# PLE gate and FFN gate/up products as seven half-size block products, with weight sums made by accumulating transfers, and the residual formed during the merge

## The chip, the core and the metric

The kernel runs on one core of a Trainium2 chip. The metric is the device time of one launch in microseconds, as a median of timed runs. The engines that matter are TensorE (PE, matrix products; its weight loads are shown as PEld), VectorE (DVE), ScalarE (ACT), GpSimd (POOL), and SyncE (SP), which here only issues transfers.

## The reference, cut to what matters

One transformer block on 512 tokens of width 1024, in fp32. After a layer norm, a gated MLP and a gated linear recurrence (HGRN2) run side by side and are merged; what the change touches is the tail:

```python
h1  = layer_norm(ALPHA * h + mix, ln1_g, ln1_b)                  # h = layer_norm(x, ln0), 512 x 1024
hid = silu(h1 @ w_ffn_gate) * (h1 @ w_ffn_up)                    # two 1024 x 2816 weights
ffn = hid @ w_ffn_down                                           # 2816 x 1024
ple = sigmoid(h1 @ w_ple_gate + b_ple_gate) * (p @ w_ple)        # 1024 x 1024 gate
out = layer_norm(ALPHA * h1 + ffn + ple, ln2_g, ln2_b)
```

## The kernel before

Each operand of a product is an exact sum of two fp32r parts, a high part h and a low part l, and each product is three matmuls (h·h, h·l, l·h). A weight arrives as a "raw" tile of 128 x 1024 values (512 KB, one SP transfer); ACT casts it to the high part (`wh`), and DVE subtracts to get the low part (`wl`). `split` does these two steps and `load_unit` the load and the split. Raw tiles have three buffers, so a load waits until an earlier tile's split is done.

The stages follow each other: the start, HGRN2, the gated MLP, the merge (`mwa`, `mwb`, `mga`, `mgb`), the output projection with layer norm 1 (`wo`, `ps_wo`), the PLE gate (`pg`, `ps_pg`), the FFN gate/up products (`fg` and `fu`, `ps_fg` and `ps_fu`) and the down product (`ps_d`) with layer norm 2. Around the change:

- LN1: the residual `r1 = ALPHA * LN0(x)` is formed on DVE at the head of the output projection, from a fresh load of x (`xr`, L676 to L680). When a token tile is normed, `turn` transposes it on PE (`ps_h`, L700) and splits it into `h1h`, `h1l`.
- PLE gate: for two column halves and four token tiles, eight k-steps of three matmuls, with 512 columns moving; 192 matmuls in all.
- FFN gate/up: the loop over m covers 256 columns of each of the two weights. `gemm_a` keeps a 128 x 128 block of weight stationary and moves 512 tokens: 48 matmuls for gate and 48 for up per m, 11 m's, 1056 matmuls. ACT makes the silu (`fsg`), DVE the product (`fhf`), and the split into `hidh`, `hidl` follows at once.
- Down: eleven k-pairs, whose operands `hidh`, `hidl` are there already.

Each engine runs its instructions in one fixed order, which a scheduler sets at build time; no engine overtakes its own queue, and that holds for the transfers that SP and POOL issue.

Of the kernel before, what the change touches and what calls it, by code (L numbers as in the profile page):

```python
# [8 lines left out]
F32 = mybir.dt.float32  # L9
F32R = mybir.dt.float32r  # L10
# [16 lines left out]
# columns of the input projection  # L27
# [4 lines left out]
def block_kernel(  # L32
# [50 lines left out]
    def gemm_a(ps, w, c0, acth, actl, name):  # L83
        """ps[:, j, :] = (act @ w[:, c0+128j : +128]).T, features on partitions"""
# [67 lines left out]
    def normed(r, mr, g, b, spread):  # L152
        """r = (r - mean) * rstd * g + b, mr: mean, rstd; spread: over three engines"""
# [7 lines left out]
    # vectors with features on partitions: 128 rows of 128 transposed at once  # L161
# [7 lines left out]
    # =============== activations that live long ===============  # L169
# [6 lines left out]
    # =============== start: PLE product, first layer norm, i of heads 0..3 ===============  # L176
# [11 lines left out]
    with tc.tile_pool(name="start", bufs=1) as sp:  # L188
# [16 lines left out]
        # p.T, split  # L205
# [23 lines left out]
        def turn0(t):  # L229
            """features on partitions, gain and bias"""  # L230
# [26 lines left out]
        # vectors  # L257
# [29 lines left out]
        # lower bound: first row of the softmax over the two rows of logits  # L287
# [15 lines left out]
    # =============== HGRN2, heads in pairs ===============  # L303
# [18 lines left out]
    # products run over chunks of 16 tokens, then over groups of 2, 4, 8 chunks  # L322
# [34 lines left out]
    def scaled(dst, src, sc, n, g, lo, hi):  # L357
        """dst = src * sc on chunks lo..hi of each group of g chunks"""
# [18 lines left out]
    def keys(m, psf):  # L377
        """forget gates, their products, decayed keys"""
# [19 lines left out]
        # suffix products need F of the chunk's tokens 1..15 only  # L398
# [4 lines left out]
        # chunk products and their products within groups  # L403
# [6 lines left out]
        fl = lambda ap: ap.rearrange("p g c -> p (g c)")  # noqa: E731  # L410
# [56 lines left out]
    def scores(m):  # L467
        """scores, [s, t] of each block of 128 tokens; states at the starts of blocks 1..3"""
# [33 lines left out]
    def outputs(m):  # L502
        """tokens on partitions, normed"""
# [56 lines left out]
    # =============== gated MLP: v, normed; the last pair of heads beside it ===============  # L560
# [6 lines left out]
    ws = gv.tile([P, NH, P], F32, name="ws")  # L567
# [6 lines left out]
    # blocks of 64 positions: a later one is not seen from an earlier one  # L574
# [27 lines left out]

    yapool_cm = tc.tile_pool(name="yapool", bufs=1, side="right")
# [33 lines left out]
    # =============== merge ===============  # L637
# [22 lines left out]
    # =============== output projection, layer norm 1, PLE gate ===============  # L660
    rpool = ctx.enter_context(tc.tile_pool(name="rpool", bufs=1))
    r1 = rpool.tile([P, TT, D], F32, name="r1")
    h1pool_cm = tc.tile_pool(name="h1pool", bufs=1)
    h1pool = h1pool_cm.__enter__()
    h1h = h1pool.tile([P, KT, T], F32R, name="h1h")
    h1l = h1pool.tile([P, KT, T], F32R, name="h1l")
    with tc.tile_pool(name="l1", bufs=1) as lp:
        g0a = load_bc(lp, ln0_g, "g0a")
        b0a = load_bc(lp, ln0_b, "b0a")
        V.tensor_scalar(out=g0a, in0=g0a, scalar1=ALPHA, scalar2=None, op0=ALU.mult)  # L670
        V.tensor_scalar(out=b0a, in0=b0a, scalar1=ALPHA, scalar2=None, op0=ALU.mult)
# [24 lines left out]
        def turn(t):  # L696
# [4 lines left out]
            ts = slice(t * P, (t + 1) * P)  # L701
            split(h1h[:, :, ts], h1l[:, :, ts], psv)

        for t in range(TT):
            for kp, us in tails:
                wo_mm(t, kp, us)
            if t > 1:
                turn(t - 2)
# [9 lines left out]
        for c in range(2):  # L718
            units = [unit_b(wpg, 2 * u, 512 * c, f"pg{c}_{u}", pool=lp if u < 2 else None, bufs=2 if u < 2 else 5,
                            eng=G if c == 0 and u else None)  # L720
                     for u in range(4)]
            for t in range(TT):
                if c == 0 and t in (1, 2):
                    turn(t + 1)
                ps = ps_tile(f"ps_pg{c}_{t}")
                for kk in range(KT):
                    h, l = units[kk // 2]
                    mm_b(ps[:, 0, :], t, h1h, h1l, kk, h, l, kk % 2, kk == 0, kk == KT - 1)
                cs = slice(512 * c, 512 * c + 512)
                sg = lp.tile([P, 512], F32, tag="sgp", name=f"sgp{c}_{t}", bufs=3)  # L730
                pl = lp.tile([P, 512], F32, tag="pl", name=f"pl{c}_{t}", bufs=2)
                nc.sync.dma_start(pl, ple_dram[:, t, cs])
                V.tensor_tensor(out=sg, in0=ps[:, 0, :], in1=bpg[:, cs], op=ALU.add)
                S.activation(sg, sg, AF.Sigmoid)
                G.tensor_tensor(out=sg, in0=sg, in1=pl, op=ALU.mult)
                V.scalar_tensor_tensor(out=r1[:, t, cs], in0=r1[:, t, cs], scalar=ALPHA, in1=sg,
                                       op0=ALU.mult, op1=ALU.add)

    # =============== FFN ===============
    with tc.tile_pool(name="hid", bufs=1, side="right") as fp:  # L740
        hidh = fp.tile([P, FT, T], F32R, name="hidh")
        hidl = fp.tile([P, FT, T], F32R, name="hidl")
        for m in range(FT // 2):
            psg = ps_tile(f"ps_fg{m}")
            gemm_a(psg, wg, 256 * m, h1h, h1l, f"fg{m}")
            psu = ps_tile(f"ps_fu{m}")
            gemm_a(psu, wu, 256 * m, h1h, h1l, f"fu{m}")
            for a in range(2):
                f = 2 * m + a
                sg = fp.tile([P, T], F32, tag="fsg", name=f"fsg{f}", bufs=2)  # L750
                S.activation(sg, psg[:, a, :], AF.Silu)
                hf = fp.tile([P, T], F32, tag="fhf", name=f"fhf{f}", bufs=2)
                V.tensor_tensor(out=hf, in0=psu[:, a, :], in1=sg, op=ALU.mult)
                split(hidh[:, f, :], hidl[:, f, :], hf)
        h1pool_cm.__exit__(None, None, None)

        with tc.tile_pool(name="fin", bufs=1) as lp:
            g2 = load_bc(lp, ln2_g[0], "g2")
            b2 = load_bc(lp, ln2_b[0], "b2")
            acc = [ps_tile(f"ps_d{t}") for t in range(TT)]  # L760
            NP, TAIL = FT // 2, 2
# [66 lines left out]
```

## Time and profile before

| | |
|---|---|
| median of 3 runs | 996.57 us (995.71 to 997.85) |
| span of the profiled execution | 992.0 us |
| PE busy | 963.9 us, 97% of the span, 4745 matmuls |
| DVE busy | 474.0 us, 48% |
| ACT busy | 289.6 us, 29% |
| POOL busy | 132.0 us, 13% |
| bytes moved | 104.60 MB, mean 105 GB/s |

The profiled execution carries no time of its own beside its span; the runs' median lies 4.6 us above that span, which is what lies around it. Busy PE includes waiting inside the pipeline, so the share says that PE seldom lacks work, not that each matmul is at its peak.

### The profile page before, as it was taken

The numbers are of one execution on the slowest core, as the hardware profiler recorded it, in microseconds if no ns is written. First come the engines' busy times: TensorE is split into PE (matmuls) and PEld (weight loads), VectorE is DVE, ScalarE is ACT, GpSimd is POOL, SyncE is SP. The second block draws the span as 40 slices with busy tenths as digits, with TensorE's granted clock in tenths as the row PEclk, the third lists the DMA queues.
The fourth block names the chain that finished last, engine by engine and source line by source line (L and its number), as shares of the span: only waits on it lengthen the run. The fifth ranks groups of instructions, "written<-read, shape, count | busy, mean of one in ns | idle before, by whom it ended". The sixth has DMA issues, their size and how long they took to land.

```text
span 992.0 us, 11393 instructions
## 1 busy us (share of the span) xinstructions
PE 963.9 (97%) x4745; PEld 795.3 (80%) x4745; DVE 474.0 (48%) x538; ACT 289.6 (29%) x335; POOL 132.0 (13%) x106
## 2 busy tenths in 40 slices
PE   6999999998999999999999989999999999999996
PEld 5788878787888888888888868888888888888885
DVE  6667935767249543332324984333323333311307
ACT  4244222333324332232322222332223223212301
POOL 5314410505006000000000332000000000000004
PEclk9999999999999999999999999999999999999999
DMA  8343223225222423333235425333332333322302
GB/s 288 127 138 107 65 81 90 64 65 167 66 65 85 128 77 94 95 97 102 89 106 216 166 81 153 98 93 103 89 106 87 104 90 101 132 102 85 128 1 85
DMA packets 79939, 104.60 MB, mean 105 GB/s; under 512 B 3368, under 2 KB 60304, under 8 KB 79888
## 3 DMA queue, kind: packets, MB, share of 16 engines
q1 hardware_dynamic: 79888, 103.88, 33.4%
q8 instruction: 37, 0.61, 0.3%
q14 instruction: 14, 0.11, 0.0%
HBM read 99.67 MB, written 4.19 MB: 105 GB/s over the span
## 4 chain that ended last, share of the span: by engine, by line
PE 84%; DVE 9%; POOL 2%; DMA 2%; issue 1%; ACT 1%; SPq 0%; DVEq 0%; ACTq 0%; POOLq 0%
PE ps_fu L93 4%; PE ps_fg L93 4%; PE ps_fg L94 4%; PE ps_fu L94 4%; PE ps_fg L92 4%; PE ps_fu L92 4%; PE ps_d L99 4%; PE ps_d L98 4%; PE ps_d L100 4%; PE ps_pg L99 2%; PE ps_pg L98 2%; PE ps_pg L100 2%; PE ps_mwa L93 2%; PE ps_mwa L92 2%; PE ps_mwa L94 2%; PE ps_f L92 1%
## 5 line engine op out<-in xcount | busy, mean ns | idle before, releaser
L64 DVE TENSOR_TENSOR wl_fu<-raw_fu,wh_fu 128x1024 fp32r<-128x1024 f32 x22 | 27.0, 1225 | 88.3 <-ACT wh_fu L61 88.3
L92 PE MATMUL ps_fg<-h1h,wh_fg 128*128 128x512 f32 x176 | 68.5, 389 | 0.0
L93 PE MATMUL ps_fg<-h1l,wh_fg 128*128 128x512 f32 x176 | 68.5, 389 | 0.0
L94 PE MATMUL ps_fg<-h1h,wl_fg 128*128 128x512 f32 x176 | 68.5, 389 | 0.0
L92 PE MATMUL ps_fu<-h1h,wh_fu 128*128 128x512 f32 x176 | 68.5, 389 | 0.0
L93 PE MATMUL ps_fu<-h1l,wh_fu 128*128 128x512 f32 x176 | 68.5, 389 | 0.0
L94 PE MATMUL ps_fu<-h1h,wl_fu 128*128 128x512 f32 x176 | 68.5, 389 | 0.0
L99 PE MATMUL ps_d<-wl_d,hidh 128*128 128x512 f32 x172 | 67.8, 394 | 0.0
L98 PE MATMUL ps_d<-wh_d,hidh 128*128 128x512 f32 x172 | 67.4, 392 | 0.0
L100 PE MATMUL ps_d<-wh_d,hidl 128*128 128x512 f32 x172 | 66.7, 388 | 0.0
L139 POOL TENSOR_TENSOR mr<-mr,nhalf 128x1 f32<-128x1 f32 x12 | 12.1, 1043 | 365.7 <-DVE mr L138 365.7
L64 DVE TENSOR_TENSOR wl_d<-raw_d,wh_d 128x1024 fp32r<-128x1024 f32 x22 | 26.8, 1224 | 67.1 <-ACT wh_d L61 66.9
L61 ACT CAST wh_fu<-raw_fu 128x1024 fp32r<-128x1024 f32 x22 | 23.2, 1054 | 82.8 <-PE ps_fg L93 43.9
L61 ACT CAST wh_d<-raw_d 128x1024 fp32r<-128x1024 f32 x22 | 23.0, 1052 | 79.2 <-PE ps_d L100 52.4
L61 ACT CAST wh_fg<-raw_fg 128x1024 fp32r<-128x1024 f32 x22 | 23.2, 1055 | 75.6 <-PE ps_fu L93 39.8
L64 DVE TENSOR_TENSOR wl_fg<-raw_fg,wh_fg 128x1024 fp32r<-128x1024 f32 x22 | 26.9, 1220 | 27.4 <-ACT wh_fg L61 27.4
L64 POOL TENSOR_TENSOR wl_pg<-raw_pg,wh_pg 128x1024 fp32r<-128x1024 f32 x3 | 8.0, 2671 | 231.8 <-ACT wh_pg L61 231.8
L92 PEld LDWEIGHTS ps_fu<-h1h,wh_fu 128*128 128x128 f32 x176 | 33.0, 188 | 6.9
L92 PEld LDWEIGHTS ps_fg<-h1h,wh_fg 128*128 128x128 f32 x176 | 33.0, 188 | 6.9
L93 PEld LDWEIGHTS ps_fg<-h1l,wh_fg 128*128 128x128 f32 x176 | 33.0, 188 | 6.9
L93 PEld LDWEIGHTS ps_fu<-h1l,wh_fu 128*128 128x128 f32 x176 | 33.0, 188 | 6.9
L94 PEld LDWEIGHTS ps_fg<-h1h,wl_fg 128*128 128x128 f32 x176 | 33.0, 188 | 6.8
(283 smaller groups left out, 2408.6 us busy)
## 6 DMA issues: line engine op xcount, KB each, us to landing
raw_fg<-in_w_ffn_gate_dram SPq DMA_DIRECT2D x22, 512.0 KB, 3.8
raw_fu<-in_w_ffn_up_dram SPq DMA_DIRECT2D x22, 512.0 KB, 3.8
raw_d<-in_w_ffn_down_dram SPq DMA_DIRECT2D x22, 512.0 KB, 3.2
raw_i<-in_w_in_dram SPq DMA_DIRECT2D x8, 512.0 KB, 5.7
raw_f<-in_w_in_dram SPq DMA_DIRECT2D x8, 512.0 KB
raw_q<-in_w_in_dram SPq DMA_DIRECT2D x8, 512.0 KB, 3.8
raw_g<-in_w_in_dram SPq DMA_DIRECT2D x8, 512.0 KB, 4.1
raw_v<-in_w_in_dram SPq DMA_DIRECT2D x8, 512.0 KB, 3.8
```

The costliest lines, as they stand in the source:

```text
L61: S.copy(h, src)
L64: (eng or V).tensor_tensor(out=l, in0=src, in1=h.bitcast(F32), op=ALU.subtract)
L92: PE.matmul(ps[:, j, :], h[:, k, cs], acth[:, kk, :], start=first, stop=False)
L93: PE.matmul(ps[:, j, :], h[:, k, cs], actl[:, kk, :], start=False, stop=False)
L94: PE.matmul(ps[:, j, :], l[:, k, cs], acth[:, kk, :], start=False, stop=last)
L98: PE.matmul(ps, acth[:, kk, ts], h[:, k, :], start=first, stop=False)
L99: PE.matmul(ps, acth[:, kk, ts], l[:, k, :], start=False, stop=False)
L100: PE.matmul(ps, actl[:, kk, ts], h[:, k, :], start=False, stop=last)
L139: G.tensor_tensor(out=dst, in0=dst, in1=nhalf[:, 0:n], op=ALU.pow)
```

## The change

A product of a 2 x 2 block matrix of activations with a 2 x 2 block matrix of weights needs eight block products in the plain way. `strassen` makes it with seven, of sums of blocks. The activation sums (`combine`) are formed once, when h1 is transposed. The weight sums are formed anew for each set of weight blocks, in place, by transfers that POOL issues and that add to their target: `t += u`, `u += b22`, then `t += b22` when the first sum in t has been split, then `t += b21` when the second has been split. So one tile t carries three sums (t1, t2, t4) one after another. The four tiles t, u, b22, b21 come from a pool of eight buffers, `wx`; block b11 has a raw buffer and is loaded once more as the start of t. For the FFN the blocks are: k halves by gate/up columns (256 columns each per m) for the weights, token halves by k halves for the activations; each of the seven products is 24 matmuls with 256 tokens moving. For the PLE gate a product is 24 matmuls with 512 columns moving for each token tile pair.

Further: the residual is formed in the merge loop (`residual`, with ACT and POOL); `hid` stays fp32 and is split pair by pair in the down stage (`hid_pair`), two pairs' buffers ahead and more; the tile `ws` of the gated MLP moves to a raw buffer.

```diff
+    def strassen(wx, src, name, order, prod, evac):
+        def load(us, n, pool=wx, bufs=8):
+            ts = [pool.tile([P, *u.shape[1:]], F32, tag="raw", name=f"{n}_{name}_{i}", bufs=bufs)
+                  for i, u in enumerate(us)]
+            for t, u in zip(ts, us):
+                nc.sync.dma_start(t, u)
+            return ts
+        def add(ts, us):
+            for t, u in zip(ts, us):
+                G.dma_start(t, u, accum_op=ALU.add)
+        def parts(n, xs):
+            return [wparts(x, f"{name}_{n}{i}") for i, x in enumerate(xs)]
+        b11 = load(src[0][0], "b11", wpool, 3)
+        t = load(src[0][0], "t")
+        u = load(src[0][1], "u")
+        b22 = load(src[1][1], "b22")
+        b21 = load(src[1][0], "b21")
+        add(t, u)
+        add(u, b22)
+        for p in order.split():
+            if p == "X":
+                prod("X", parts("11", b11), "11", True, True)
+                evac("p1")
+            elif p == "W":
+                prod("W", parts("21", b21), "12", True, True)
+                evac("c11")
+            elif p == "Z":
+                prod("Z", parts("t1", t), "s1", True, False)
+                add(t, b22)
+                evac("z5")
+            elif p == "Y":
+                prod("Y", parts("t2", t), "a6", True, False)
+                add(t, b21)
+                evac("y6")
+            elif p == "Z2":
+                prod("Z", parts("22", b22), "a3", False, True)
+                evac("c12")
+            elif p == "Y2":
+                prod("Y", parts("t3", u), "a7", False, False)
+                evac("c22")
+            elif p == "Y3":
+                prod("Y", parts("t4", t), "22", False, True)
+                evac("c21")
+    def product_a(bank, units, a, first, last):
+        (h, l), = units
+        ah, al = a
+        for j in range(2):
+            o = bank[:, HT * j:HT * j + HT]
+            cs = slice(j * P, (j + 1) * P)
+            for k in range(4):
+                PE.matmul(o, h[:, k, cs], ah[:, k, :], start=first and j == 0 and k == 0, stop=False,
+                          skip_group_check=True)
+                PE.matmul(o, h[:, k, cs], al[:, k, :], start=False, stop=False, skip_group_check=True)
+                PE.matmul(o, l[:, k, cs], ah[:, k, :], start=False, stop=last and j == 1 and k == 3,
+                          skip_group_check=True)
...
-    ws = gv.tile([P, NH, P], F32, name="ws")
+    ws = wpool.tile([P, NH, P], F32, tag="raw", name="ws", bufs=3)
...
+        def residual(t):
+            r = r1[:, t, :]
+            nc.sync.dma_start(r, xv[:, t, :])
+            S.activation(r, r, AF.Identity, scale=mr0[:, t, 1:2], bias=nmr[:, t, :])
+            G.tensor_tensor(out=r, in0=r, in1=g0a, op=ALU.mult)
+            G.tensor_tensor(out=r, in0=r, in1=b0a, op=ALU.add)
...
-        for t in range(TT):
-            xr = lp.tile([P, D], F32, tag="xr", name=f"xr{t}", bufs=2)
-            nc.sync.dma_start(xr, xv[:, t, :])
-            V.scalar_tensor_tensor(out=xr, in0=xr, scalar=mr0[:, t, 0:1], in1=g0a, op0=ALU.subtract, op1=ALU.mult)
-            V.scalar_tensor_tensor(out=r1[:, t, :], in0=xr, scalar=mr0[:, t, 1:2], in1=b0a, op0=ALU.mult, op1=ALU.add)
...
+            strassen(wx, [[src_b(wpg, 4 * a, 4, 512 * b) for b in range(2)] for a in range(2)], "pg",
+                     "X W Z Y Z2 Y2 Y3", pg_prod, pg_evac)
...
+            strassen(wx, [[src_a(w, 4 * a, 256 * m) for w in (wg, wu)] for a in range(2)], f"f{m}",
+                     "X Z Y Z2 Y2 W Y3", prod, evac)
...
+        def hid_pair(kp):
+            h = lp.tile([P, 2, T], F32R, tag="hidh", name=f"hidh{kp}", bufs=4)
+            l = lp.tile([P, 2, T], F32R, tag="hidl", name=f"hidl{kp}", bufs=4)
+            split(h, l, hid[:, 2 * kp:2 * kp + 2, :])
+            return h, l
```

What the scheduler makes of this on POOL, in the middle of the FFN (f2, f3, f4 are the m's). Before, POOL has no work between the last product of the PLE gate and layer norm 2:

```order
L735 TENSOR_TENSOR sgp1_2_4325<-sgp1_2_4325,pl1_2_4326 128x512
L735 TENSOR_TENSOR sgp1_3_4357<-sgp1_3_4357,pl1_3_4358 128x512
L139 TENSOR_TENSOR mr2_0_6449<-mr2_0_6449,nhalf_71 128x1
```

Of the changed kernel, POOL, the two periods that follow each other there; each row is one adding transfer, target on the left:

```order
L175 DMA t_f3_0_5121<-u_f3_0_5123 128x1024
L175 DMA u_f3_0_5123<-b22_f3_0_5125 128x1024
L175 DMA t_f2_0_4891<-b22_f2_0_4895 128x1024
L175 DMA t_f2_0_4891<-b21_f2_0_4897 128x1024
L175 DMA t_f4_0_5351<-u_f4_0_5353 128x1024
L175 DMA u_f4_0_5353<-b22_f4_0_5355 128x1024
L175 DMA t_f3_0_5121<-b22_f3_0_5125 128x1024
L175 DMA t_f3_0_5121<-b21_f3_0_5127 128x1024
```

The second and third sums of one m stand behind both first sums of the next m. On SP the loads of the changed kernel stand so, one period:

```order
L169 DMA b11_f4_0_5349<-in_w_ffn_gate_dram 128x4x256
L169 DMA t_f3_0_5121<-in_w_ffn_gate_dram 128x4x256
L169 DMA u_f3_0_5123<-in_w_ffn_up_dram 128x4x256
L169 DMA b22_f3_0_5125<-in_w_ffn_up_dram 128x4x256
L169 DMA b21_f3_0_5127<-in_w_ffn_gate_dram 128x4x256
L169 DMA b11_f5_0_5579<-in_w_ffn_gate_dram 128x4x256
```

Before, there were four loads a period, and one queue of raw buffers; now there are five, and t of one m takes the buffer that t of two m's before leaves. Last, DVE at the end of the FFN in the changed kernel (`g0`, `u0`: gate and up of the first token half, `g1`, `u1` of the second):

```order
L944 TENSOR_TENSOR hid_4423<-u0_10_6861,g0_10_6921 128x2x256
L938 TENSOR_TENSOR g1_10_6953<-p1_10_6769,ps_f10_b_6728 128x512
L65 TENSOR_TENSOR wl_d2_0_7102<-raw_d2_0_7099,wh_d2_0_7101 128x1024
L944 TENSOR_TENSOR hid_4423<-u1_10_6891,g1_10_6953 128x2x256
L65 TENSOR_TENSOR hidl0_6984<-hid_4423,hidh0_6983 128x1024
L65 TENSOR_TENSOR hidl1_7048<-hid_4423,hidh1_7047 128x1024
```

The first split of `hid` for the down stage stands behind the last product of the FFN; before, `hidh` and `hidl` of the early m's were made many m's ahead.

## Rows read from the trace of the kernel before

**Rows 1.** The page: busy time of each engine, then the chain that ended last, by engine.

```profile
PE 963.9 (97%) x4745; PEld 795.3 (80%) x4745; DVE 474.0 (48%) x538; ACT 289.6 (29%) x335; POOL 132.0 (13%) x106
...
PE 84%; DVE 9%; POOL 2%; DMA 2%; issue 1%; ACT 1%; SPq 0%; DVEq 0%; ACTq 0%; POOLq 0%
```

**Rows 2.** Windows: stretch, length, busy time by engine (instructions), granted clock, DMA share, GB/s.

```profile
543.60:571.30 27.70, 27.70 (x126) 22.56 (x124) 26.85 (x28) 6.22 (x6) 8.45 (x4) 1.00 0.52 177
571.30:575.00 3.70, 0.05 (x1) 0.00 (x0) 3.70 (x4) 0.00 (x0) 2.58 (x2) 0.95 0.02 4
575.00:621.70 46.70, 46.68 (x208) 38.15 (x209) 30.18 (x37) 14.30 (x17) 12.45 (x9) 0.97 0.41 124
862.90:983.90 121.00, 121.00 (x529) 98.98 (x527) 38.59 (x49) 23.40 (x26) 7.88 (x8) 1.00 0.25 83
367.00:543.60 176.60, 176.60 (x775) 145.00 (x774) 58.92 (x50) 46.00 (x50) 0.00 (x0) 1.00 0.34 110
655.00:861.00 206.00, 206.00 (x910) 170.62 (x910) 68.16 (x74) 59.52 (x76) 0.00 (x0) 1.00 0.33 97
574.60:578.40 3.80, 3.38 (x13) 2.77 (x14) 3.77 (x7) 1.38 (x2) 1.46 (x1) 0.55 0.40 138
```

**Rows 3.** Waits of PE: what waited for what, us in total, times, longest.

```profile
PE ps_h L700 <- DVE r L159: 3.7, 1, 3.7
PE ps_ws L573 <- DMA raw_v<-in_w_in_dram: 2.5, 1, 2.5
```

**Rows 4.** Waits of SP's transfer queue from 600 to 860 us.

```profile
SPq L69 <- DVE wl_fu L64: 109.3, 22, 7.5
SPq L69 <- DVE wl_fg L64: 96.5, 21, 5.3
```

**Rows 5.** The chain that ended last: start, us, instruction.

```profile
239.42 8.07 DMA raw_v<-in_w_in_dram
247.53 1.94 PE ps_ws L573 x8
249.47 0.43 PE ps_v L98
249.90 0.43 PE ps_v L99
250.32 0.32 PE ps_v L100
251.09 0.23 PE ps_v L100
...
322.15 1.78 PE ps_mx L614 x16
...
551.63 3.39 DVE xr L679
555.05 1.28 DVE r L680
...
572.36 2.62 DVE r L159
575.02 1.97 PE ps_h L700 x8
...
583.17 0.87 PE ps_h L700 x8
```

**Rows 6.** The tile raw_fg: its load, cast and subtraction (ns: shortest, median, longest).

```profile
L69 SPq DMA_DIRECT2D raw_fg<-in_w_ffn_gate_dram x22: 367/368/368, 589.9 to 810.9; - x22
L61 ACT CAST wh_fg<-raw_fg x22: 1048/1054/1058, 594.3 to 824.8; 128x1024 fp32r<-128x1024 f32 x22
L64 DVE TENSOR_TENSOR wl_fg<-raw_fg,wh_fg x22: 1215/1220/1226, 595.4 to 825.9; 128x1024 fp32r<-128x1024 f32 x22
...
DMA to landing us min/median/max: 3.6/3.8/5.5
```

**Rows 7.** Transfers: kind, count, KB each, median us from issue to landing.

```profile
raw_d<-in_w_ffn_down_dram SPq DMA_DIRECT2D x22, 512.0 KB, 3.2
...
b_v<-in_b_in_dram SPq DMA_DIRECT2D x1, 512.0 KB, 4.3
gmg<-in_gm_norm_g_dram SPq DMA_DIRECT2D x1, 512.0 KB, 5.2
gmb<-in_gm_norm_b_dram SPq DMA_DIRECT2D x1, 512.0 KB, 6.0
```

**Rows 8.** Groups of instructions from 540 to 992 us: busy us, mean ns, idle before.

```profile
L753 DVE TENSOR_TENSOR fhf<-ps_fu,fsg 128x512 f32<-128x512 f32 x22 | 14.2, 686 | 36.9 <-PE ps_fu L94 36.9
L751 ACT ACTIVATE fsg<-ps_fg 128x512 f32<-128x512 f32 x22 | 11.8, 590 | 0.0
L679 DVE SCALAR_TENSOR_TENSOR xr<-xr,mr,g0a 128x1024 f32<-128x1024 f32 x4 | 9.5, 2386 | 3.3 <-DMA xr<-in_x_dram 3.3
L680 DVE SCALAR_TENSOR_TENSOR r<-xr,mr,b0a 128x1024 f32<-128x1024 f32 x4 | 5.1, 1285 | 0.1
```

More of the change, by code (lines that the diff above doesn't have):

```diff
@@ L19 @@
 TT = T // P
+HT = T // 2
 DFF = 2816
@@ new lines, in wparts @@
+    def wparts(x, name):
+        a, b = x.shape[1:]
+        h = wpool.tile([P, a, b], F32R, tag="wh", name=f"wh_{name}", bufs=5)
+        l = wpool.tile([P, a, b], F32R, tag="wl", name=f"wl_{name}", bufs=5)
+        split(h, l, x)
+        return h, l
[42 more added lines that the diff above has]
+                evac("c21")
@@ new lines, in product_b @@
+    def product_b(banks, units, a, first, last, t):
+        ah, al = a
+        ts = slice(t * P, (t + 1) * P)
+        n = 2 * len(units)
+        for kk in range(n):
+            h, l = units[kk // 2]
+            k = kk % 2
+            o = banks[:, t, :]
+            PE.matmul(o, ah[:, kk, ts], h[:, k, :], start=first and kk == 0, stop=False, skip_group_check=True)
+            PE.matmul(o, ah[:, kk, ts], l[:, k, :], start=False, stop=False, skip_group_check=True)
+            PE.matmul(o, al[:, kk, ts], h[:, k, :], start=False, stop=last and kk == n - 1, skip_group_check=True)
@@ L121, in row_bc, with src_b, src_a @@
+    def src_b(w, k0, nk, c0):
+        return [w[(k0 + 2 * u) * P:(k0 + 2 * u + 2) * P, c0:c0 + 512].rearrange("(k p) c -> p k c", p=P)
+                for u in range(nk // 2)]
+    def src_a(w, k0, c0):
+        return [w[k0 * P:(k0 + 4) * P, c0:c0 + 256].rearrange("(k p) c -> p k c", p=P)]
     def row_bc(vec, n):
@@ L700, in turn @@
                 PE.transpose(psv[:, k, :], r1[:, t, k * P:(k + 1) * P], ident)
-            ts = slice(t * P, (t + 1) * P)
-            split(h1h[:, :, ts], h1l[:, :, ts], psv)
+            f = h1f[:, :, t * P:(t + 1) * P]
+            S.copy(f, psv)
+            if t < 2:
+                ts = slice(t * P, t * P + P)
+                for n, fs in (("11", f[:, 0:4, :]), ("12", f[:, 4:8, :])):
+                    split(comb[n][0][:, :, ts], comb[n][1][:, :, ts], fs)
+            else:
+                combine(comb, cpool, h1f, slice((t - 2) * P, (t - 1) * P))
         for t in range(TT):
@@ L717, in block_kernel @@
         yapool_cm.__exit__(None, None, None)
[L718 to L721, printed above, removed]
-            for t in range(TT):
[L723 to L728, printed above, removed]
-                cs = slice(512 * c, 512 * c + 512)
[L730 to L737, printed above, removed]
@@ new lines, in block_kernel, with up, prod, new @@
+    fpool_cm = tc.tile_pool(name="hid", bufs=1, side="right")
+    fpool = fpool_cm.__enter__()
+    hid = fpool.tile([P, FT, T], F32, name="hid")
+    with tc.tile_pool(name="up", bufs=1) as fp:
+        def up(m):
+            psa, psb = ps_tile(f"ps_f{m}_a"), ps_tile(f"ps_f{m}_b")
+            bank = {"X": psa[:, 0, :], "Z": psa[:, 1, :], "Y": psb[:, 0, :], "W": psb[:, 1, :]}
+            v = {n: b.rearrange("p (a c) -> p a c", c=HT) for n, b in bank.items()}
+            t = {}
+            def prod(chain, units, n, first, last):
+                product_a(bank[chain], units, comb[n], first, last)
+            def new(n, bufs=1):
+                t[n] = fp.tile([P, 2, HT], F32, tag=n, name=f"{n}_{m}", bufs=bufs)
+                return t[n]
+            def evac(n):
+                if n == "p1":
+                    S.copy(new("p1", 2), v["X"])
+                elif n in ("y6", "z5"):
+                    V.tensor_tensor(out=new(n), in0=v[n[0].upper()], in1=t["p1"], op=ALU.subtract)
+                else:
+                    i, j = int(n[1]) - 1, int(n[2]) - 1
+                    x, y, op = {"c11": (v["W"], "p1", ALU.add), "c22": (v["Y"], "z5", ALU.add),
+                                "c12": (v["Z"], "y6", ALU.add), "c21": (v["Y"], "p1", ALU.subtract)}[n]
+                    o = new(f"{'gu'[j]}{i}")
+                    if n == "c21":
+                        V.tensor_tensor(out=o, in0=t[y], in1=x, op=op)
+                    else:
+                        V.tensor_tensor(out=o, in0=x, in1=t[y], op=op)
+                    if j == 0:
+                        S.activation(o, o, AF.Silu)
+                    if f"g{i}" in t and f"u{i}" in t:
+                        V.tensor_tensor(out=hid[:, 2 * m:2 * m + 2, HT * i:HT * i + HT],
+                                        in0=t[f"u{i}"], in1=t[f"g{i}"], op=ALU.mult)
+            strassen(wx, [[src_a(w, 4 * a, 256 * m) for w in (wg, wu)] for a in range(2)], f"f{m}",
+                     "X Z Y Z2 Y2 W Y3", prod, evac)
+        for m in range(FT // 2):
+            up(m)
```

179 lines of the change are left out of this document (115 added, 64 removed).

## The prediction

> **What bounds the kernel now.** I read the busy shares and the chain first. PE is busy in 963.9 of 992.0 us and carries 84% of the chain that ended last, DVE only 9% [rows 1]. Then the windows, one for each stage that the change touches [rows 2]. From 655 to 861 us (FFN gate/up) PE is busy in all of 206.00 us with 910 matmuls: 0.2264 us each, at full clock, while DVE has 68.16, ACT 59.52 and POOL nothing. So the 1056 matmuls of this stage take 1056 × 0.2264 = 239.1 us, 21.7 per m. The reader should see that nothing is waited for here, and that SP's queue is held back by buffers for over 200 us [rows 4]: transfers have slack. The waits of PE show two gaps near the change [rows 3]: 3.7 us before the transposes `ps_h` (waiting for the norm `r` on DVE) and 2.5 us before `ps_ws`. After the first the clock is low: 0.55 over 574.60 to 578.40 [rows 2], near the lower of its two levels (1.2 of 2.4 GHz); after the second the matmuls `ps_v` take 0.43, 0.43, 0.32 instead of 0.23 us, and eight transposes 1.94 instead of 0.87 us [rows 5].
>
> **FFN, work of PE.** Seven products of 24 matmuls with 256 columns stand for 96 with 512, so 168 for 96 per m. A matmul with 256 columns is not in the trace. Bounds: below, `ps_mx` with 128 columns and weights of its own for each matmul, x16 in 1.78 us, 0.111 each [rows 5]; above, the 0.2264 of 512 columns. From half of 0.2264 plus some 7 ns I take 0.120: `ps_mx` shows that weights can follow each other that fast, so the upper bound is far off. 168 × 0.120 = 20.2 us per m (18.6 by the lower bound), 222 us for the stage. If nothing else bounds, that is −17.
>
> **FFN, the loop of transfers.** This is the term that decides. In POOL's order the second and third sums of one m (t += b22, t += b21) stand behind both first sums of the next m (t += u, u += b22). And the first sum of the next m but one needs the buffer that t leaves when its third sum has been split. That closes a loop with a period of one m:
>
> 1. t's buffer comes free; SP issues t, then u, back to back. A load lands after 3.8 us [rows 6]. The second lands later: of three transfers issued back to back the landing times are 4.3, 5.2, 6.0 though each was issued some 0.4 later (an issue is 0.367) [rows 6, 7], so each further 512 KB adds 0.4 + 0.9 = 1.3. Together 5.1 us.
> 2. t += u lands: A. The next add, u += b22, may not write u while t += u still reads it, and it holds POOL's queue: so A plus about 0.4 for an issue.
> 3. t += b22 of the earlier m lands: A, plus what u += b22 in front of it moves.
> 4. Its split: cast 1.05 and subtraction 1.22 [rows 6], 2.3.
> 5. t += b21 lands: A. Split again: 2.3. The buffer is free.
>
> The period is 5.1 + 0.4 + 3A + 4.6 plus the add in front, that is 10.1 + 3A + f. An accumulating transfer of 512 KB from SBUF to SBUF is not in the trace. Below, a plain load of that size among few others: 3.2 (`raw_d` [rows 7]), with f = 0.9; that gives 20.6, which is PE's own 20.2. Above, `raw_v` behind three other loads, 8.07 [rows 5], which gives over 34. Between them I reason that an add must read its target too, so it moves one more 512 KB: 3.2 + 1.3 = 4.5, with f = 2 × 0.9 = 1.8. That gives 10.1 + 13.5 + 1.8 = **25.4 us**, above PE's 20.2.
>
> The Trainium skill speaks against the change here: "Collectives: The Full Stack", section "The bandwidth ceiling: the fold count and why AG ≠ RS ≠ AR", says that an add in the transfer path needs two source reads, two read descriptors for a chunk, and so gets about half a copy's rate. No run here shows it yet; by it the period would be the 25.4 just worked out. The page "DMA: Bandwidth & Descriptors", section "Anatomy of one DMA — SWDGE (gpsimd) path", gives 2.0 us plus bytes/436e3, an estimate of 3.2 us for 512 KB; by that the period would be 20.6 and the stage bound by PE.
>
> A second view of the same: four loads per m make a DMA share of 0.33 now [rows 2], 0.33 × 21.7 / 4 = 1.8 us for each 512 KB. After, five loads and four adds are 9 × 1.8 = 16.2 us a period if an add counts once, 13 × 1.8 = 23.4 if it counts twice. Transfers lose their slack either way.
>
> For the stage: nine such periods link the third sum of the first m to that of the tenth. Outside lie about 14 of the 77 products of 24 × 0.120 = 2.88 us: two ahead of the first, and twelve behind the last (seven of the last m, and five that PE is behind the splits, whose weight buffers are five). Nine periods + 40.3 us. At 25.4 that is 268.9, **+30** against 239.1. Break-even is (239.1 − 40.3)/9 = 22.1, where A is 3.4 to 3.7, by f.
>
> **PLE gate.** 24 matmuls with 512 columns fewer, 24 × 0.2264 = −5.4. The xr and r work leaves DVE: 9.5 + 5.1 us [rows 8], in a stretch where DVE is busy in 26.85 of 27.70 us [rows 2] and the chain runs through it (3.39 and 1.28 [rows 5]). So the gap of 3.7 and the low clock behind it (3.8 × 0.45 = 1.7) should go. Against it: nine more weight subtractions on DVE instead of POOL or not there at all (9 × 1.22 = 11), two calls of `combine` (four additions of 512 elements and five subtractions each, at 0.69 by `fhf` [rows 8], 12.4), and eight middle results (5.5), less two low parts of h1 (2.4). DVE had 30.18 in this stage of 46.70 [rows 2] and comes to some 56 us where PE now wants 41. The 14.6 us freed on DVE ahead of it take up about as much if the work can be done early, nothing if it can't: a stall between 0 and 15, and I take 7. Sum −5.4 − 5.4 + 7 = **−4**.
>
> **FFN to down.** Before, PE passed from one to the other without a gap. Now the first split of `hid` stands behind the last product on DVE. In series: subtraction from PSUM 0.69, silu 0.59, product 0.69 [rows 8], cast 1.05, and 1.22 for the low part [rows 6], with a weight's subtraction of 1.22 between: 5.5 us, of which the low part's share (the third matmul needs it) is partly covered. Some 4.5 of idle PE and 1.7 of low clock: **+6**. The eleven splits of the down stage (2.3 a pair) lie beside 11 us of PE a pair, where DVE has 38.59 of 121.00 [rows 2].
>
> **The rest.** The load of `ws` moves ahead of the first raw_v and its wait of 2.5 goes, with 1.07 of slow transposes and 0.5 of slow matmuls: **−4**. The residual in the merge costs nothing: ACT has 46.00 of 176.60 there and POOL 0.00 [rows 2]. Without that cover it would be the 14.6 us that DVE loses.
>
> **Sum.** The durations are those of one execution with a span of 992.0; runs have 996.57, and I take the 4.6 as constant. 996.6 + 30 − 4 + 6 − 4 = **1024**.
>
> **Rivals.** Faster: the adds cost one pass or the loop is looser than I read it, so that PE bounds. For it speaks the slack of SP's queue [rows 4] and the lower bound of A. Against it, nine transfers a period in place of four, with three adds in series behind each other and two splits. It decides where the period falls below 22.1. With PE as the bound: 996.6 − 17 − 4 + 6 − 4 = **977**; with no stall in the gate, 970. Same: an add of the load's 3.8 with f = 0.9 has a period of 22.4, +3, in all **997**. Slower still: adds queue behind the five loads on the same engines, A = 5.5 (a load's longest landing [rows 6]) and f = 1.8: 28.4, +57, in all **1051**. That the matmul with 256 columns saves nothing (168 × 0.2264 = 38 us a period, +179) would need the opposite of what `ps_mx` shows; I give it 0.02.
>
> **How the numbers follow.** What a measurement here tells from no change is 0.2%, 2 us. Adds of two passes near 1024: 0.42. PE-bound, near 977: 0.28. Near 997: 0.10, of which half within 0.2% and the rest shared. Queued adds, 1051 and beyond: 0.18. Small matmuls that save nothing: 0.02. Faster 0.30, same 0.05, slower 0.65. The range takes in the PE-bound case with some of its tail, and the queued adds up to A near 6: 972 to 1058. The likeliest case's own range is 1010 to 1042 (A from 4.0 to 5.1).
>
> **What would show it.** Right: in the FFN PE waits once or twice a period for DVE's `wl_..t2`, `wl_..t4`, and these for the adds; the waits of ACT's casts of t name POOL's transfers; landing times of the adds near 4.5; PE busy about 0.8 of the stage; matmuls of 256 columns 0.12 apart. In the gate DVE is nearly always busy, the gaps before `ps_ws` and `ps_h` are gone, and one of some 4.5 us stands before the first `ps_d`. Wrong: PE at 97% in the FFN with 20 us a period (adds faster than 3.4), or a gate in which PE waits for DVE by more than 15 us.

## The result, and the profile after

The changed kernel takes 1051.65 us (median of 4 runs, 1049.92 to 1052.00) against 997.21 for the kernel before: a ratio of 1.0553, 95% interval 1.0533 to 1.0572, slower by 55 us. The forecast was slower, at 1024 with a range of 972 to 1058. The sign and the place are right; the forecast loss of 27 us is half of the measured one. The profiled execution has a span of 1048.2 us against 992.0, so 56.2 us are to be found in the trace.

First the page of the changed kernel: busy time of each engine, the transfer queues, and the chain by engine and line.

```profile
PE 967.4 (92%) x5513; PEld 834.4 (80%) x5513; DVE 567.1 (54%) x648; ACT 346.2 (33%) x390; POOL 197.1 (19%) x159
...
q1 hardware_dynamic: 86176, 110.69, 32.9%
q0 software_dynamic: 7488, 27.27, 14.7%
...
PE 18%; DMA 13%; DVE 3%; ACT 2%; issue 2%; POOL 0%; DVEq 0%; POOLq 0%; ACTq 0%
DMA t_f<-b_f 8%; DMA t_f<-u_f 5%; PE ps_d L99 4%; PE ps_d L100 4%; PE ps_d L101 4%; PE ps_f_b L223 2%; ACT wh_f_t L62 2%; DVE wl_f_t L65 2%; PE ps_f_b L220 2%; PE ps_f_b L222 2%; DVE hid L944 0%; POOL u_f L175 0%; DVE y L931 0%; PE ps_f_a L223 0%; PE ps_f_a L220 0%
```

The chain is followed back only to 646.92 us, so its shares sum to 38%, where PE alone stood for 84% before [rows 1]. By line the adding transfers `t_f<-b_f` and `t_f<-u_f` now head it; by engine DMA has 13%, and PE 18%, most of it in the down product behind the FFN. The queue of POOL's transfers, 27.27 MB, holds the engines for 14.7% of their time; SP's, with four times the bytes, for 32.9%.

The windows of the stages (the columns are those of [rows 2]): output projection and gate; the FFN; a stretch of it in which PE does not wait; the passage to the down product.

```profile
522.70:623.20 100.50, 93.19 (x417) 75.48 (x416) 71.51 (x93) 36.74 (x43) 22.98 (x16) 0.97 0.70 190
623.20:914.30 291.10, 243.88 (x1826) 238.38 (x1824) 149.32 (x169) 99.03 (x112) 40.56 (x42) 0.88 0.71 164
742.00:753.00 11.00, 11.00 (x97) 11.00 (x96) 6.84 (x8) 4.25 (x5) 0.95 (x2) 1.00 1.00 268
914.30:918.50 4.20, 0.16 (x2) 0.00 (x0) 2.53 (x4) 2.67 (x4) 0.00 (x0) 1.00 0.47 136
```

In the FFN PE idles 47 us of 291, and its clock is 0.88 of full speed on average. Where it does not wait, 97 matmuls of 256 columns take 11.00 us, 0.113 each. The waits of PE say what it idles for:

```profile
PE ps_f_b L220 <- ACT wh_f_t L62: 39.2, 10, 5.6
PE ps_f_b L223 <- DVE wl_f_t L65: 5.5, 9, 1.0
...
PE ps_d L99 <- ACT hidh L62: 4.0, 1, 4.0
...
PE ps_h L835 <- DVE r L285: 2.9, 1, 2.9
PE ps_pgZ L235 <- ACT cs1h L62: 1.9, 1, 1.9
```

Ten times in eleven m's the product Y waits for the cast of the second sum in t; a wait for the cast of the fourth sum stands nowhere in the list. The transfers' landing times (columns as in [rows 7]) are longer than forecast:

```profile
t_f<-b_f POOLq DMA_DIRECT2D x22, 512.0 KB, 6.1
...
u_f<-in_w_ffn_up_dram SPq DMA_DIRECT2D x11, 512.0 KB, 6.1
t_f<-u_f POOLq DMA_DIRECT2D x11, 512.0 KB, 6.4
...
u_f<-b_f POOLq DMA_DIRECT2D x11, 512.0 KB, 5.1
t_pg<-b_pg POOLq DMA_DIRECT2D x4, 512.0 KB, 4.6
```

An add of the PLE gate, where no other transfer runs beside three of the four, lands after 4.6 us, the 4.5 of the prediction. In the FFN it is 6.1 to 6.4.

Now one period of the FFN. POOL's timeline (start, us it holds POOL's queue, the transfer, idle before and its releaser):

```profile
752.93 0.87 POOL L175 DMA_DIRECT2D u_f<-b_f  x1 [6.32 <-DMA t_f<-u_f]
753.47 1.22 POOL L175 DMA_DIRECT2D t_f<-b_f  x1
762.86 0.89 POOL L175 DMA_DIRECT2D t_f<-b_f  x1 [8.17 <-DVE wl_f_t L65]
773.26 0.87 POOL L175 DMA_DIRECT2D t_f<-u_f  x1 [9.51 <-DVE hid L944]
780.10 0.86 POOL L175 DMA_DIRECT2D u_f<-b_f  x1 [5.96 <-DMA t_f<-u_f]
780.64 1.20 POOL L175 DMA_DIRECT2D t_f<-b_f  x1
```

The loads that SP issues in between, and DVE's subtractions (the first one is that of the first sum in t):

```profile
763.62 0.37 SPq L169 DMA_DIRECT2D t_f<-in_w_ffn_gate_dram  x1
765.35 0.37 SPq L169 DMA_DIRECT2D u_f<-in_w_ffn_up_dram  x1
768.74 0.37 SPq L169 DMA_DIRECT2D b_f<-in_w_ffn_up_dram  x1
771.98 2.70 SPq L169 DMA_DIRECT2D b_f<-in_w_ffn_gate_dram  x2
```

```profile
748.03 1.22 DVE L65 TENSOR_TENSOR wl_f_t<-t_f,wh_f_t 128x1024 fp32r<-128x1024 f32 x1 [0.60 <-ACT wh_f_t L62]
...
761.23 1.23 DVE L65 TENSOR_TENSOR wl_f_t<-t_f,wh_f_t 128x1024 fp32r<-128x1024 f32 x1 [10.74 <-ACT wh_f_t L62]
762.37 1.22 DVE L65 TENSOR_TENSOR wl_f<-b_f,wh_f 128x1024 fp32r<-128x1024 f32 x1
...
764.11 1.22 DVE L65 TENSOR_TENSOR wl_f_t<-u_f,wh_f_t 128x1024 fp32r<-128x1024 f32 x1
...
770.72 1.23 DVE L65 TENSOR_TENSOR wl_f_t<-t_f,wh_f_t 128x1024 fp32r<-128x1024 f32 x1 [0.29 <-ACT wh_f_t L62]
```

The period is 780.64 − 753.47 = 27.2 us; over the eight from 639.32 to 855.66 it is 27.04. And each load starts when one subtraction ends: t at 763.62 when b22's ends (762.37 + 1.22), u at 765.35 when that of u's sum ends (764.11 + 1.22), the last block at 771.98 when that of the fourth sum in t ends. These three starts follow their subtractions by 0.03 us, and so do those of t and u in all nine periods from 630 to 848 us. So the next t does not take the buffer that t leaves, as the prediction and the section on the change had it: t takes that of b22, u that of u, b22 that of b21, and b21 that of t. The adding transfer t += u at 773.26 follows u's load. What the view names as its releaser, `hid` on DVE, stands nowhere among its operands. That gives two theories for the loop:

- **A**, the prediction's: the fourth sum and its split stand in it; three adds in series.
- **B**: second sum lands (753.47 to 760.15, 6.7 us); t's, b22's and u's splits (to 765.35, 5.2); u's load until the add is issued (to 773.26, 7.9); that add, then u += b22, then the next second sum, which stands behind them in POOL's queue (to 780.64, 7.4). Sum 27.2, with two adds; the fourth sum lies beside it. As means of seven periods the four steps are 7.0, 5.2, 7.2 and 7.7.

In B the second sum is held back by its place in the queue: the first sum in t was split at 749.25, and `t += b22` was issued at 753.47, 4.2 us later.

### The profile page after: what moved, and what is told of

The parts are those of the page before. It is cut to its first block, busy times and chain, and to the rows that moved or that the text cites. A ratio compares the mean times of both kernels' runs of the same rounds, so it can differ in the third digit from the quotient of the medians.

```text
span 1048.2 us, 13353 instructions
## 1 busy us (share of the span) xinstructions
PE 967.4 (92%) x5513; PEld 834.4 (80%) x5513; DVE 567.1 (54%) x648; ACT 346.2 (33%) x390; POOL 197.1 (19%) x159
## 3 DMA queue, kind: packets, MB, share of 16 engines
q1 hardware_dynamic: 86176, 110.69, 32.9%
q0 software_dynamic: 7488, 27.27, 14.7%
## 5 line engine op out<-in xcount | busy, mean ns | idle before, releaser
L65 DVE TENSOR_TENSOR wl_f_t<-t_f,wh_f_t 128x1024 fp32r<-128x1024 f32 x33 | 40.4, 1224 | 116.1 <-ACT wh_f_t L62 115.9
L62 ACT CAST wh_f_t<-t_f 128x1024 fp32r<-128x1024 f32 x33 | 34.6, 1049 | 136.2 <-DMA t_f<-b_f 99.5
L220 PE MATMUL ps_f_b<-ca6h,wh_f_t 128*128 128x256 f32 x88 | 30.8, 350 | 39.2 <-ACT wh_f_t L62 39.2
L99 PEld LDWEIGHTS ps_d<-wh_d,hidh 128*128 128x128 f32 x172 | 32.9, 191 | 11.2 <-ACT hidh L62 4.2
L175 POOL DMA_DIRECT2D t_f<-b_f x22 | 22.4, 1018 | 99.8 <-DVE wl_f_t L65 99.8
L65 DVE TENSOR_TENSOR wl_f<-b_f,wh_f 128x1024 fp32r<-128x1024 f32 x33 | 40.2, 1217 | 0.1
L487 POOL TENSOR_TENSOR k<-sgm,lv 128x512 f32<-128x512 f32 x8 | 15.5, 1960 | 123.5 <-DVE lv L539 123.5
L100 PEld LDWEIGHTS ps_d<-wl_d,hidh 128*128 128x128 f32 x172 | 32.7, 190 | 6.8
L101 PEld LDWEIGHTS ps_d<-wh_d,hidl 128*128 128x128 f32 x172 | 32.4, 189 | 6.8
L62 ACT CAST wh_f<-b_f 128x1024 fp32r<-128x1024 f32 x33 | 34.3, 1040 | 1.2 <-ACT g L942 0.8
L220 PE MATMUL ps_f_b<-c22h,wh_f_t 128*128 128x256 f32 x88 | 31.2, 354 | 0.9 <-DVE g L940 0.9
L222 PE MATMUL ps_f_b<-c22l,wh_f_t 128*128 128x256 f32 x88 | 30.6, 348 | 0.0
```

What stands on the lines that cost most here:

```text
L62: S.copy(h, src)
L65: (eng or V).tensor_tensor(out=l, in0=src, in1=h.bitcast(F32), op=ALU.subtract)
L99: PE.matmul(ps, acth[:, kk, ts], h[:, k, :], start=first, stop=False)
L100: PE.matmul(ps, acth[:, kk, ts], l[:, k, :], start=False, stop=False)
L101: PE.matmul(ps, actl[:, kk, ts], h[:, k, :], start=False, stop=last)
L175: G.dma_start(t, u, accum_op=ALU.add)
```

## The experiments

**Without the fourth sum.**

```diff
                 prod("Y", parts("t2", t), "a6", True, False)
-                add(t, b21)
+                if name == "pg":
+                    add(t, b21)
```

> The fourth weight sum (t += b21) of every FFN m is left out, so the last product of each m uses the third sum again; nothing else is taken away. Theory A (the loop of the prediction: t's buffer is given back by the split of the fourth sum, three adds in series): the period of the FFN falls from 27.0 us by an add and a split, to PE's own 20 or so, and the whole run to 985 to 995 us. Theory B (the changed kernel's buffers show that u's load takes the buffer that u leaves at the split of its sum, which stands behind the split of t's second sum; two adds and a load in series, the fourth sum beside them): the period stays at 25 to 27 us, the run at 1030 to 1050.

Measured: 1038.1 us (one run). Two of the adds t += u, with seven periods between them, 25.7 each:

```profile
663.37 0.85 POOL L175 DMA_DIRECT2D t_f<-u_f  x1 [15.70 <-DVE y L932]
...
843.61 0.89 POOL L175 DMA_DIRECT2D t_f<-u_f  x1 [17.99 <-DVE y L932]
```

Theory A falls: the fourth sum is not in the loop, although the changed kernel's chain of waits goes through it in some periods (its transfer at 791.48 us, for one). What its absence gives is 1.3 us a period. The means of B's four steps are 7.2, 5.2, 5.6 and 7.7 in this run, so the gain lies in u's load (7.2 before). That fits the changed kernel's transfers: from 764.5 to 767.5 us the fourth sum holds all of the engines' time and SP's queue 5% of it, and only from 768.5 on does SP's queue, with t's and u's loads, hold them all.

**Copies for adds.**

```diff
-                G.dma_start(t, u, accum_op=ALU.add)
+                G.dma_start(t, u)
```

> Each adding transfer becomes a plain copy between the same tiles on the same queue, so the weight sums are left out and the output is not the reference's. If an add costs more because it reads its target too, a copy lands after 3.5 to 4.5 us where an add took 6.4, and the FFN period falls to 21 to 23 us by theory B (two transfers in the loop), to PE's 20 by theory A (three): the run at 1000 to 1012 or at 985 to 995. If the way from POOL's queue is what costs, copies land after 6 us as well and the run stays at 1045 to 1052.

Measured: 1000.4 us (one run), a period of 22.1 (655.27 to 810.03 us, seven). Of its page the queues, and its landing times:

```profile
q0 software_dynamic: 7488, 27.27, 7.0%
...
t_f<-b_f POOLq DMA_DIRECT2D x22, 512.0 KB, 3.8
t_f<-u_f POOLq DMA_DIRECT2D x11, 512.0 KB, 5.8
u_f<-b_f POOLq DMA_DIRECT2D x11, 512.0 KB, 2.9
t_pg<-b_pg POOLq DMA_DIRECT2D x4, 512.0 KB, 2.9
```

One of its periods on POOL's timeline:

```profile
728.31 0.53 POOL L175 DMA_DIRECT2D t_f<-b_f  x1
...
743.46 0.53 POOL L175 DMA_DIRECT2D t_f<-u_f  x1 [8.06 <-DMA u_f<-in_w_ffn_up_dram]
...
749.79 0.53 POOL L175 DMA_DIRECT2D t_f<-b_f  x1
```

The same packets and bytes hold the engines 7.0% of 998.7 us, 70 us; as adds 14.7% of 1048.2, 154 us: 2.2 times as long. SP's queue holds them for 345 us in either run (32.9% and 34.6%), so this is the adds' own price and not that of a fuller system. A copy alone lands after 2.9 where the add took 4.6. The prediction's price of about two passes is shown. The period fell by 4.9 us, to where theory B put it; the means of its steps are 4.4, 5.2, 5.7 and 6.8, so some 3.5 of this are the two transfers in the loop and 1.6 are u's load. The fall by itself would not tell two adds from three, since three times 4.6 − 2.9 is 5.1; that is told by the run before.

**No adds.**

```diff
-                G.dma_start(t, u, accum_op=ALU.add)
+                pass
```

> All the adding transfers are left out (the weight sums with them). Both theories: PE bounds the FFN at 168 x 0.115 = 19.4 us an m, 80 us less than measured, so 965 to 980 us for the run. If something else in the seven-product form bounds (DVE's splits, PSUM), it stays above 1000.

Measured: 973.0 us (one run). Its window in the FFN:

```profile
640.00:820.00 180.00, 180.00 (x1556) 180.00 (x1555) 123.18 (x139) 81.19 (x93) 0.00 (x0) 1.00 0.40 121
```

PE never waits, at full clock, 0.1157 us a matmul, 19.4 an m. This is what the seven products are worth here if their sums were free: 23 us below the kernel before, of which half has nothing to do with them, as the run with the residual and ws alone shows below.

**Sums on POOL.**

```diff
-                G.dma_start(t, u, accum_op=ALU.add)
+                G.tensor_tensor(out=t, in0=t, in1=u, op=ALU.add)
```

> The weight sums are made by POOL's own additions (128 x 1024, some 2.7 us each as vn and wl_pg took before) in place of the transfers; all else is as in the changed kernel. Theory B: load 6, two or three additions in series and two splits make 19 to 20 us a period, PE's own: 975 to 990 us. Rival: DVE is slowed beside POOL (the norm r took 2.62 us beside a POOL subtraction where it takes 1.28 alone), its 14 us of work an m come to 20 or more: 1000 to 1030.

Measured: 1019.4 us, a ratio to before of 1.0230 (1.0213 to 1.0247): the rival's range. DVE's subtractions in the FFN of this run, then its window:

```profile
L65 DVE TENSOR_TENSOR wl_f<-b_f,wh_f 128x1024 fp32r<-128x1024 f32 x27 | 52.8, 1956 | 0.0
L65 DVE TENSOR_TENSOR wl_f_t<-t_f,wh_f_t 128x1024 fp32r<-128x1024 f32 x27 | 43.0, 1593 | 33.3 <-ACT wh_f_t L62 33.3
...
650.00:850.00 200.00, 182.20 (x1502) 178.18 (x1502) 157.98 (x134) 78.51 (x90) 97.80 (x36) 0.98 0.38 111
```

The same subtraction takes 1.22 us in the changed kernel. Beside POOL's additions it takes 1.6 to 2.0, and DVE's work of 13.3 us an m (123.18 us for 1556 matmuls in the run with no adds) becomes 17.7 of a period of 22.4 (1502 matmuls in 200 us). That is not the whole of it: DVE is still free for a fifth of the window, and B's loop stands here too, with steps of 2.4, 6.9, 4.8 and 8.3 us. Slower subtractions lengthen its splits from 5.2 to 6.9. Another 9 us of the run are lost ahead of the FFN (106.6 us for output projection and gate, against 97.6).

**POOL's order.**

```diff
-        add(t, u)
-        add(u, b22)
+        if name[0] == "f" and name != "f0":
+            with tc.issue_after(behind["t2"]):
+                add(t, u)
+            with tc.issue_after(behind["t4"]):
+                add(u, b22)
...
-                add(t, b22)
+                behind["t2"] = add(t, b22)
...
-                add(t, b21)
+                behind["t4"] = add(t, b21)
```

POOL's queue then has, for f3 and f4:

```order
L177 DMA t_f3_0_5121<-b22_f3_0_5125 128x1024
L177 DMA t_f4_0_5351<-u_f4_0_5353 128x1024
L177 DMA t_f3_0_5121<-b21_f3_0_5127 128x1024
L177 DMA u_f4_0_5353<-b22_f4_0_5355 128x1024
```

> The changed kernel with the same adding transfers, and POOL's order alone changed: t += u of the next m is issued behind the second sum of this m and not ahead of it, u += b22 of the next m behind the fourth. Theory B (the second sum stands behind adds that wait for u's load of the next m): the loop of 27.0 us opens, what is left in series is an add, a split and an add's issue, some 12 to 16 us, so PE bounds again at 20 to 21 us a period: 975 to 995 us. Theory C (the transfers' share of the engines is what bounds, 0.71 of a period of 27 us is 19 us, and they slow each other as they come closer): the period comes down to 23 to 25 only, 1010 to 1035.

Measured: 999.1 us, a ratio of 1.0028 (1.0014 to 1.0042). The transfers and their bytes are those of the changed kernel; their order alone gives back 52 of the 55 us. Window and landing times:

```profile
640.00:840.00 200.00, 189.28 (x1553) 183.62 (x1552) 121.27 (x140) 79.28 (x92) 32.56 (x37) 0.99 0.88 212
...
t_f<-u_f POOLq DMA_DIRECT2D x11, 512.0 KB, 8.2
u_f<-b_f POOLq DMA_DIRECT2D x11, 512.0 KB, 9.2
```

The period is 200 / 1553 × 168 = 21.6 us. Theory B holds for the most part. The result lies between its range and theory C's: the transfers are now in use for 0.88 of the time, the first two adds of an m land after 8.2 and 9.2 us (the other two after 5.7), and the last 2 us a period may be theirs; no run shows that alone.

**Half the sums on POOL, in the new order.** As the run before, with `add_pool` (POOL's addition) for the second and fourth sums.

> As the run with POOL's order changed, and the second and fourth sums of each m (and of the PLE gate) made by POOL's own additions, 2.6 us each, in place of transfers; the first and third stay transfers. Theory B: PE bounds, 975 to 990 us. If transfers bound (theory C), this has half of them and is the faster one of the two by 20 us or more. If DVE beside POOL's additions bounds (its subtractions took 1.6 to 2.0 us with four POOL additions an m), it has half of that: DVE at 16 to 17 us an m stays below PE's 20.

Measured: 984.3 us, a ratio of 0.9872 (0.9855 to 0.9889), faster than the kernel before. In the FFN PE is busy in all of a window, so it bounds again:

```profile
640.00:840.00 200.00, 200.00 (x1715) 199.81 (x1715) 149.68 (x156) 89.46 (x102) 67.79 (x39) 0.99 0.65 164
```

**The residual and ws alone**, in the kernel before, with no seven products.

```diff
-    ws = gv.tile([P, NH, P], F32, name="ws")
+    ws = wpool.tile([P, NH, P], F32, tag="raw", name="ws", bufs=3)
...
+        for m in range(KT // 2):
+            residual(m)
```

> The kernel before with two parts of the change alone: the move of ws and the residual formed in the merge; no seven-product form, no weight sums. By the prediction's terms: -4 for ws and -5.4 for the gap ahead of the PLE gate with its low clock, 985 to 989 us. If the residual on ACT and POOL costs something in the merge, or the gap ahead of the gate stays (it was 2.9 us in the changed kernel), 990 to 994.

Measured: 985.6 us, a ratio of 0.9885 (0.9868 to 0.9902). Windows of the merge from 363.80 us, and of the output projection with the gate:

```profile
363.80:523.50 159.70, 159.70 (x700) 131.10 (x700) 56.95 (x43) 41.83 (x47) 17.42 (x6) 1.00 0.33 102
523.50:615.10 91.60, 91.60 (x417) 75.17 (x416) 53.04 (x65) 25.81 (x28) 22.76 (x14) 1.00 0.40 127
```

PE waits in neither, and among all its waits in this run none is at `ps_ws` or `ps_h`. So the residual is hidden in the merge, and both gaps with their low clock are gone. The prediction's 9.4 us for these two parts became 11.

**A plain gate in the changed kernel.** The block between `pch = {}` and the FFN is replaced by the plain loops of before; `turn` splits the blocks 21 and 22 as well.

```diff
+                        PE.matmul(ps[:, 0, :], ah[:, kk % 4, ts], h[:, k, :], start=kk == 0, stop=False)
+                        PE.matmul(ps[:, 0, :], ah[:, kk % 4, ts], l[:, k, :], start=False, stop=False)
+                        PE.matmul(ps[:, 0, :], al[:, kk % 4, ts], h[:, k, :], start=False, stop=kk == KT - 1)
```

> The changed kernel with its PLE gate made again by plain products (192 matmuls in place of 168, the sums of blocks of h1 still formed there for the FFN); the FFN, its sums and POOL's rule as in the changed kernel. The stage from the output projection's first matmul to the gate's last took 97.6 us in the changed kernel without the FFN's 24 small matmuls in it, 91.6 in the run that has the residual and ws alone. If the seven products of the gate lose more to DVE than they save on PE, this run is 3 to 6 us faster than the changed kernel, 1045 to 1049; if the sums for the FFN are what costs there, it is 2 to 6 us slower, 1053 to 1058.

Measured: 1042.05 us, a ratio of 1.0484 (1.0451 to 1.0516): 7 us faster than the changed kernel by the ratios, 9.6 by the medians, more than expected, and elsewhere. By the starts of matmuls in the timelines (us; the 24 small matmuls that the FFN puts into the gate are taken as 2.8 and counted with the FFN):

| run | output projection and gate | FFN | FFN to down |
|---|---|---|---|
| before | 96.9 | 239.4 | 0.2 |
| changed | 97.6 | 293.9 | 4.3 |
| no adds | 97.9 | 216.6 | 4.3 |
| sums on POOL | 106.6 | 252.6 | 4.3 |
| POOL's order | 99.3 | 240.7 | 4.3 |
| half on POOL | 103.9 | 221.6 | 4.3 |
| residual and ws alone | 91.6 | 239.4 | 0.2 |
| plain gate | 99.3 | 283.8 | 4.3 |
| half on POOL, plain gate | 99.4 | 220.1 | 4.3 |

The gate did not get shorter (99.3 against 97.6), the FFN did. The gate's seven products fill the eight buffers of `wx`, so in the changed kernel the second m's t += u is issued at 615.29 and the third's at 639.32 us. With a plain gate the first two m's have their first sums long before the gate (t += u at 517.86 and 528.27 us). PE's waits in that stage of this run:

```profile
PE ps_h L836 <- DVE r L285: 6.0, 1, 6.0
```

Neither of the two expectations was right. In this run the wait is for the norm of the fourth token tile, at 586.96 us. DVE is busy in all of 562 to 587 us, and between the third and the fourth norm it forms and splits the sums of blocks of h1. In the changed kernel the wait is 2.9 us, for the third tile, and no such sum stands ahead of it yet: the first one starts at 578.40 us. There DVE subtracts for two weights (570.91 to 573.26) before it finishes the norm.

**Half the sums on POOL, plain gate.** The last two together.

> The run with POOL's order changed and half of the sums on POOL, with the PLE gate by plain products as well. Its stage up to the gate's last matmul took 106.7 us there, so if the gate's seven products (with POOL's sums beside DVE) are what costs, it falls to 92 to 97 us, and the run from 984 to 970 to 976, below the run with the residual and ws alone. If not, 980 to 990.

Measured: 978.4 us, a ratio of 0.9829 (0.9812 to 0.9845), the fastest here of those that form all the sums; 2 us above the range expected, since the stage fell to 99.4 and not to 92 to 97, for the same wait (6.1 us before `ps_h`). Against the run with the residual and ws alone the seven products of the FFN bring 6 to 7 us (by the ratios and by the medians).

## Why the prediction was right and wrong, step by step

The terms, in us of the span, by the table and the starts of `ps_wo` and `ps_d`:

| term | predicted | measured |
|---|---|---|
| ws | −4 | −3.7 (first `ps_wo` at 526.4, then 522.7) |
| output projection and gate | −4 | +0.7 |
| FFN | +30 | +54.5 |
| FFN to down | +6 | +4.1, and +0.6 of low clock behind it |
| sum | +28 | +56.2 |

The step that failed is the loop of transfers in the FFN: the prediction had its members wrong and took the transfers in it at prices that hold when little else runs. The runs show a loop of two adds, three splits and u's load, with steps of 7.0, 5.2, 7.2 and 7.7 us, closed by POOL's order. Two smaller steps failed beside it: the two ends of the FFN, 49.8 us in place of 40.3, and the low clock behind the gate's waits, which the prediction took as gone.

- **The direction** followed from the right argument: POOL's order closes a loop over transfers that is longer than PE's 20 us. The experiment on POOL's order shows it, 52 us from the order alone.
- **The loop's members** were wrong: "the first sum of the next m but one needs the buffer that t leaves when its third sum has been split". t takes b22's buffer and u takes u's; the loop has two adds, not three, and three splits between (theory B; shown by the run without the fourth sum and by the start times of the loads). PE waits for the second sum, as the prediction expected, and never for the fourth, which it expected too.
- **The size of A** was wrong in its place. 4.5 us is what an add takes alone (4.6 measured). In the loop an add takes 6.1 to 6.4 median and up to 8.05, and u's load 7.2 in the mean to the add behind it in place of 5.1: five loads and four adds share the engines, whose share is 0.71 over the stage, and a load gets little of them while an add runs. With the prediction's own prices theory B's loop would have been 6.3 + 5.2 + 5.1 + 5.4 = 22.0 us, no loss. So two errors offset each other, an add too many and prices too low, and that the 25.4 came so near the measured 27.0 is luck. The rival with queued adds (A = 5.5, 1051) gave the measured time by luck too: its loop is the same wrong one, and it priced only adds held up by loads, where loads are held up by adds as well.
- **Periods and ends.** From t += b21 of the first m (issued at 630.01 us) to that of the tenth (874.11), nine periods take 244.1 instead of 228.6, +15.5. The rest of the stage took 49.8 instead of 40.3, +9.5: 9.7 ahead of these periods in place of 5.8, and 40.1 behind them in place of 34.6. The prediction let the FFN's first sums be ready at the gate's end, and overlooked that the gate's tiles hold the pool. With the plain gate the same nine periods take 237.7 and the rest 46.1, together the 10 us by which the FFN is shorter there. Of the 46.1, 39.6 lie behind the periods; so the end of the stage is longer than in the working with either gate, and why is open.
- **Small matmuls**: 0.1157 against 0.120 taken.
- **The gate**: the 5.4 of fewer matmuls is there, but "the gap of 3.7 and the low clock behind it should go" failed. The gap went from the second token tile to the third (2.86 us before `ps_h` at 574.60, and a mean clock of 0.81 from there to 582.00): the changed gate transposes the third tile after its first 12 matmuls, where the kernel before had 24, and DVE's two weight subtractions stand ahead of the norm. Further on PE waits 4.4 us in all for the casts and splits of `combine`'s sums and of a weight sum (products Z and Y of the gate). Together PE idles 7.3 us in this stage, about the stall of 7 that the prediction took. What it left out is the low clock behind these waits: by the granted clock some 3.3 us from 567.30 to 615.00 (an estimate: 0.96 over 7.3 us, 0.81 over 7.4, 0.95 over 33), where it took the 1.7 of before as gone. With the residual alone the gap does go: 91.6 against 96.9.
- **FFN to down**: the mechanism was right; 4.0 us of wait for `hidh`, and 0.6 of low clock behind it in place of 1.7.

The Trainium skill, "Collectives: The Full Stack", section "The bandwidth ceiling: the fold count and why AG ≠ RS ≠ AR", says that an add in the transfer path needs two source reads. The traces agree with about half a copy's rate, 2.2 times a copy's time on the engines here; the reads themselves no run shows. The estimate of 3.2 us from the Trainium skill, "DMA: Bandwidth & Descriptors", section "Anatomy of one DMA — SWDGE (gpsimd) path", is near what a copy takes alone, 2.9 measured; for an add it is too small by 1.4.

What stays open: that DVE's order is what makes a norm late, by 2.9 us with the seven products (third tile) and by 6 with the plain gate (fourth tile), was read from the timelines, not tried. A pool of more than eight buffers, which might open the loop as well, was not tried either. And of the last 2 us a period in the run with POOL's order, that they are the transfers' is argued from the run with half the sums on POOL, which also changes DVE's load.

## What to carry to other kernels

Work moved to transfers is not free when it is in series: count the loop over buffers and queues, with each transfer at its landing time under the load that the change itself makes, and look at which buffer each load really takes. Before giving up such a change, look at the issuing engine's queue: an add that waits for a load of the next m held back one that was ready, and a change of their order alone gave back 52 of 55 us. A chain of waits that runs through an instruction does not prove that it is in the loop; taking that instruction away does.

## What the runs showed of the hardware

- An adding transfer of 512 KB between SBUF tiles costs the transfer engines 2.2 times a copy (154 against 70 us for the same 27.27 MB), lands after 4.6 us alone, and after 5.7 to 9.2 (medians of the four sums) in the run where the engines are in use for 0.88 of the time; it holds POOL's queue for 0.87 us where SP's issue takes 0.37.
- While an adding transfer runs, loads issued beside it get little: from 764.5 to 767.5 us of the changed kernel POOL's queue holds all of the engines' time and SP's 5%; from 766.0 to 767.5, with two loads waiting, 11%.
- DVE's subtraction of 128 x 1024 takes 1.22 us, and 1.6 to 2.0 beside POOL's additions of the same shape; with half of these additions 1.2 to 1.6.
- Matmuls of 256 columns with weights of their own follow each other at 0.1157 us, half the 0.2264 of 512 columns.
